# A two-block fp32 model on one core: LRU weights split one product ahead, pairs of second-memory products in one bank, attention tables built in the LRU, priority for the last norm tile, mask products of 64 columns

## The chip, the cores and the metric

The kernel runs as one program on one core of a Trainium2 chip and computes a whole two-block model with a batch of one. The metric is the device time of one execution in microseconds (us), median of three runs. TensorE is called PE in the profile, VectorE DVE, ScalarE ACT, GpSimd POOL, and the queue that issues most loads SP.

## What is computed

The input has 1024 tokens of 1024 values. The first block is a mixer (spatial gating, a state-space branch, attention to a memory), a residual and a layer norm. The second block is the part that matters here:

```python
h = rms_norm(x, norm_mix)
lru_in, lru_gate, q, k, v, g_lru, g_attn = split(h @ w_in)
xc = causal_depthwise_conv(lru_in, conv_w, conv_b)
hr = rg_lru(xc, lru_wa, lru_ba, lru_wx, lru_bx, lru_lambda)   # a scan over the tokens
y_lru = (gelu(lru_gate) * hr) @ w_lru_o
o_attn = diff_attention(q, k, v, cos, sin, ...)               # 8 heads, 2 maps each
x = x + (sigmoid(g_lru) * y_lru + sigmoid(g_attn) * (o_attn @ w_attn_o)) @ w_out
x = x + memory_cross_attention_2(x, mem, ...)                 # kv = rms_norm(mem) @ w_ckv
x = x + hierarchical_moe(rms_norm(x, norm_ffn), ...)
```

In `diff_attention` queries and keys are normed per head and partly rotated by tables `cos` and `sin`, and a query sees the keys of its own chunk of 64 tokens and of all chunks before it. Query tiles have 128 tokens, so in the last key tile the first 64 queries must not see the last 64 keys.

## The kernel before, in words

Every product is kept near fp32 by a split: an operand is rounded into a high part on ACT (`Copy` to fp32r) and the rest is taken on DVE (`x - hi`), and `mm3` (L172 to L176) makes three matmuls of it: high by high, and the two mixed ones. `stream` and `load_split` load a weight by SP into a raw buffer (a ring of two in the LRU), and `split` (L168) makes `wh` on ACT and `wl` on DVE; `wh` and `wl` have four buffers each.

The program is written stage by stage, and the tile framework's scheduler orders the instructions of each engine by priority and by when it expects their inputs. The order in the code is the priority, unless `high_priority` raises it or `behind` lowers it; `issue_after` adds an order against a named instruction. Each engine then runs its list strictly in that order, and waits at an instruction whose inputs are late.

Three stages are touched.

- `ln1` (L957). Eight token tiles: product, residual, layer norm, the second block's first norm (`xnt`), then `finish()` transposes the tile on PE (L949) and splits it into `xnh` and `xnl`. The last two tiles are finished after the loop. All later products read `xnh` and `xnl`.
- `lru` (L1037). Eight channel blocks c. For each, `proj` makes two products of 48 matmuls of 512 columns: `w_li` of the next block, and `w_lgate` of this one. Then come the gate products (`pg`, with `w_lg2`), tanh, exp and sqrt on ACT, and the scan on DVE. In `proj` the weight is loaded and split when its product is written, so just ahead of it. Between the blocks the generator `mem2` (L1671) advances by one step: it makes keys and values of the second memory by eight products of 24 matmuls with 256 columns (`w_ckv`, four column blocks n, two token tiles t), each in a PSUM tile `pj` of the pool `pm2`, which has one buffer. ACT evicts each to `kn` (keys, n below 2) or `kv` (values). Keys are normed and transposed back on PE into a tile `pt` that shares that one buffer (L1697). The memory itself is split into `mh` and `ml` by eight ACT and eight DVE instructions, which are ordered behind `ln_end`, the last square and the last scaling of `ln1`.
- `attention` (L1166). At its start POOL builds the two rotation tables `rot` (L1174 to L1184, five instructions each), POOL and DVE fill the mask operands `ma` and `mb` (L1190 to L1193), and PE makes the first key and value products. `norm_rope` norms on DVE (`nr`), takes two products with `rot` (`rp`), and `transposed` puts the result through PE (L1249). `unit_qk` makes the scores of one query tile, head and map: matmuls L1487 and L1488, then a mask matmul L1490 that adds a large negative number. It writes 256 columns, of which 64 are not zero; there are 4 x 8 x 2 x 2 = 128 of them.

```python
            def proj(src, w=None):
                w = w or self.stream(W, src, [128, 8, 128])
                ps = PJ.tile([128, 2, 512], F32, name="pj", tag="pj")
...
        for n in range(4):
            w = [self.stream(W, A["w_ckv"][n, j], [128, 4, 256]) for j in range(2)]
            for t in range(2):
                ps = PS.tile([128, 2, 128], F32, name="pj", tag="pj")
```

Of the kernel before, what the change touches and what calls it, by code (L numbers as in the profile page):

```python
# [11 lines left out]
F32 = mybir.dt.float32  # L12
F32R = mybir.dt.float32r
BF = mybir.dt.bfloat16
# [9 lines left out]
LN_EPS = 1e-5  # L24
# [105 lines left out]
class Model:  # L130
# [813 lines left out]
    def transpose_split(self, src, PT, hi, lo):  # L944

        for q in range(2):
# [3 lines left out]
            self.split(hi[:, 4 * q:4 * q + 4], lo[:, 4 * q:4 * q + 4], pt)  # L950
# [6 lines left out]
    def ln1(self):  # L957
# [4 lines left out]
        with self.pool("lnw1") as LW, self.pool("lny", side="right") as NW, self.pool("ln", side="right") as N, self.pool("lnps", bufs=2, space=PSUM) as PO, \  # L962
# [3 lines left out]
            def finish():  # L966
                i, xn = last.pop(0)
                self.transpose_split(xn, PT, self.xnh[:, :, i * 128:(i + 1) * 128],
                                     self.xnl[:, :, i * 128:(i + 1) * 128])
# [18 lines left out]
            for i in range(8):  # L988
# [17 lines left out]
                r = N.tile([128, 2, 512], F32, name="r", tag="r")  # L1006
                st = N.tile([128, 2, 6], F32, name="st", tag="st", bufs=2)
                for n in range(2):
                    self.stt(r[:, n], xr[:, n * 512:(n + 1) * 512], ALPHA, ps[:, n], OP.mult, OP.add)
                    nc.vector.bn_stats(out=st[:, n], in_=r[:, n])  # L1010
                if i < 6:
                    nxx.append(load_x(i + 2))
                mv = N.tile([128, 8], F32, name="mv", tag="mv", bufs=2)
                nc.vector.bn_aggr(out=mv[:, 0:2], in_=st)
                self.ts(mv[:, 2:3], mv[:, 1:2], LN_EPS, OP.add)
                self.rsqrt(mv[:, 3:4], mv[:, 2:3], 1)
                r1 = r.rearrange("p a b -> p (a b)")
                self.ts(r1, r1, mv[:, 0:1], OP.subtract, mv[:, 3:4], OP.mult)
                x1 = N.tile([128, 1024], F32, name="x1t", tag="x1t")
                self.tt(x1, r1, lg, OP.mult)  # L1020
                self.tt(x1, x1, lb, OP.add, nc.vector if i == 7 else nc.gpsimd)
                nc.gpsimd.dma_start(out=self.x1[i], in_=x1)
                xn = N.tile([128, 1024], F32, name="xnt", tag="xnt", bufs=2)
                sq = self.act(xn, x1, AF.Square, accum=mv[:, 4:5])
                self.ts(mv[:, 5:6], mv[:, 4:5], 1.0 / 1024, OP.mult, EPS, OP.add)
# [1459 lines left out]
```

## Time and profile before

| what | value |
|---|---|
| time, median of 3 runs | 2520.61 us (2520.1 to 2521.86) |
| time of the profiled execution | 2518.23 us |
| its span in the profile | 2516.5 us |
| PE busy | 2364.3 us, 94% of the span |
| DVE, ACT, POOL busy | 1772.8, 1246.2, 504.8 us |
| `ln1`, its product to the last transposes | about 300 to 466 us |
| LRU | about 446 to 712 us |
| attention | about 712 to 1455 us |

The profiled execution has 1.7 us around its span and lies 2.4 us under the median. Matmuls are pipelined: a matmul of 512 columns is shown with 0.39 us and one of 256 columns with 0.28, but they start every 0.23 and 0.12 us, so the starts are to be read, and the idle time in brackets, not the durations. In a row of a timeline the bracket tells how long the engine had been idle and what released it. PEclk is the granted clock of TensorE in the stretch as a share of full speed; a record can stand at full or at half.

### The profile page before, as it was taken

The page shows a single profiled execution, that of the slowest core. Times are in us where ns is not written, and L with a number is a line of the kernel's source. Part 1 is how long each engine was busy: PE and PEld are TensorE (multiplying, and loading weights), DVE is VectorE, ACT ScalarE, POOL GpSimd, SP SyncE. Part 2 cuts the span into 40 slices and gives each one's busy share as a digit, 9 for nine tenths or more (in the row PEclk, how much of TensorE's full clock was granted, in tenths as well). Part 3 has the DMA queues.
Part 4 walks back from the last instruction along what each step waited for, and adds up shares of the span by engine and source line. Part 5 has one row for each costly group of instructions (what it writes and reads, how often), then busy time and mean ns, then how long its engine had stood idle before and what let it go on. Part 6 is the DMA issues. An engine that isn't in the chain of part 4 may idle for free. (4 is left out here: it accounts for less than half of the span.)

```text
span 2516.5 us, 34506 instructions
## 1 busy us (share of the span) xinstructions
PE 2364.3 (94%) x13016; PEld 1951.4 (78%) x13016; DVE 1772.8 (70%) x3221; ACT 1246.2 (50%) x1850; POOL 504.8 (20%) x362
## 2 busy tenths in 40 slices
PE   8999989989999999999899899999988999988887
PEld 6888868777889898898798778888876777666665
DVE  9667767676775666666666744236658999988887
ACT  5344532453645545455455522124435777766664
POOL 1011114100021021021121100000002333355542
PEclk9999999999999999999999999999988999999999
DMA  6322353312111111110111466532158998999995
GB/s 222 95 70 63 116 187 115 122 69 91 63 68 55 64 35 40 62 51 34 53 49 40 141 204 220 173 138 80 72 217 308 376 373 306 366 338 336 334 338 183
DMA packets 103834, 394.29 MB, mean 157 GB/s; under 512 B 14129, under 2 KB 33073, under 8 KB 79089
## 3 DMA queue, kind: packets, MB, share of 16 engines
q1 hardware_dynamic: 85008, 335.18, 37.8%
q0 software_dynamic: 18656, 56.88, 7.1%
q8 instruction: 104, 1.70, 0.3%
q14 instruction: 66, 0.53, 0.1%
HBM read 339.07 MB, written 61.31 MB: 159 GB/s over the span
## 5 line engine op out<-in xcount | busy, mean ns | idle before, releaser
L166 DVE TENSOR_TENSOR wl<-raw,wh 128x2048 fp32r<-128x2048 f32 (+2 forms) x310 | 566.0, 1839 | 120.0 <-ACT wh L154 119.6
L154 ACT ACTIVATE wh<-raw 128x2048 fp32r<-128x2048 f32 (+2 forms) x310 | 479.6, 1556 | 290.4 <-PE pj L175 87.3
L2248 POOL DMA_INDIRECT out<-y,lsti x32 | 175.2, 5475 | 331.4 <-DVE y L162 281.3
L175 PE MATMUL pg<-wl,xh 128*96 128x512 f32 x512 | 205.6, 402 | 30.1 <-DVE wl L166 29.9
L174 PE MATMUL pj<-wh,xnh 128*128 128x256 f32 x768 | 221.5, 289 | 3.2 <-ACT pc L154 2.7
L176 PE MATMUL pj<-wh,xnl 128*128 128x256 f32 x768 | 217.7, 284 | 0.0
L175 PE MATMUL pj<-wl,xnh 128*128 128x256 f32 x768 | 217.4, 283 | 0.0
L176 PE MATMUL pg<-wh,xl 128*96 128x512 f32 x512 | 201.7, 394 | 0.0
L174 PE MATMUL pg<-wh,xh 128*96 128x512 f32 x512 | 198.3, 396 | 1.0 <-ACT wh L154 1.0
L174 PEld LDWEIGHTS pj<-wh,xnh 128*128 128x128 f32 x768 | 145.4, 189 | 6.2 <-ACT pc L154 4.8
L175 PEld LDWEIGHTS pj<-wl,xnh 128*128 128x128 f32 x768 | 145.5, 189 | 0.0
L176 PEld LDWEIGHTS pj<-wh,xnl 128*128 128x128 f32 x768 | 145.3, 189 | 0.0
L179 POOL TENSOR_TENSOR ss<-ss,mhalf 128x4 f32<-128x4 f32 (+1 forms) x68 | 74.2, 1092 | 343.6 <-DVE ss L163 254.0
L175 PEld LDWEIGHTS pg<-wl,xh 128*96 128x96 f32 x512 | 82.8, 162 | 76.4 <-DVE wl L166 44.5
L154 ACT ACTIVATE e<-sc,st,ss 128x1024 f32<-128x1024 f32 (+7 forms) x128 | 105.6, 829 | 64.5 <-DVE st L158 47.6
L174 PEld LDWEIGHTS pg<-wh,xh 128*96 128x96 f32 x512 | 82.9, 162 | 37.3 <-ACT wh L154 1.4
L174 PE MATMUL pj<-xnh,wh 128*128 128x512 f32 x256 | 103.4, 405 | 7.3 <-ACT wh L154 7.0
L176 PEld LDWEIGHTS pg<-wh,xl 128*96 128x96 f32 x512 | 83.1, 162 | 32.7
L175 PE MATMUL pj<-xnl,wh 128*128 128x512 f32 x256 | 102.4, 401 | 1.3 <-DVE xnl L166 1.3
L174 PE MATMUL pg<-xnh,wh 128*128 128x512 f32 x256 | 103.1, 403 | 0.4 <-ACT kv L154 0.3
L176 PE MATMUL pj<-xnh,wl 128*128 128x512 f32 x256 | 101.9, 400 | 0.3 <-DVE wl L166 0.3
L176 PE MATMUL pg<-xnh,wl 128*128 128x512 f32 x256 | 102.1, 399 | 0.0
(997 smaller groups left out, 6429.5 us busy)
## 6 DMA issues: line engine op xcount, KB each, us to landing
raw<-in_w_gu SPq DMA_DIRECT2D x128, 1024.0 KB, 7.7
raw<-in_w_dn SPq DMA_DIRECT2D x64, 1024.0 KB, 9.6
raw<-in_w_out SPq DMA_DIRECT2D x16, 512.0 KB, 4.5
ta<-tg POOLq DMA_DIRECT2D x32, 256.0 KB, 2.4
t<-ta SPq DMA_DIRECT2D x14, 512.0 KB, 4.3
raw<-in_w_ga SPq DMA_DIRECT2D x12, 512.0 KB, 3.5
raw<-in_w_v SPq DMA_DIRECT2D x12, 512.0 KB, 3.4
xraw<-in_xT SPq DMA_DIRECT2D x8, 512.0 KB, 8.9
```

Source lines behind the costliest of these rows:

```text
L154: return self.nc.scalar.activation(out=out, in_=in_, func=func, **kw)
L166: return (eng or self.nc.vector).tensor_tensor(out=out, in0=a, in1=b, op=op)
L174: mm(ps, l[0], r[0], start=start, stop=False)
L175: mm(ps, l[0], r[1], start=False, stop=False)
L176: mm(ps, l[1], r[0], start=False, stop=stop)
L179: self.nc.gpsimd.tensor_tensor(out=out, in0=in_, in1=self.mhalf[:, :w], op=OP.pow)
L2248: return nc.gpsimd.indirect_dma_start(out=self.out, out_offset=bass.IndirectOffsetOnAxis(ap=u["row"], axis=0), in_=u["y"], in_offset=None, ...
```

## The change

1. LRU: `proj` takes its weight from a list and first starts the load and split of the next one, so each weight is split a whole product ahead.
2. `mem2`: the two token tiles of a block n share one PSUM tile (`pair`) of 2 x 256 columns in the one buffer; the transposes `pt` move to the pool of the gate products, which has three buffers.
3. `attn_const` is called in block c = 1 of the LRU and not after it, and now builds the first table (`rot[1]`, for keys) and the mask operands too; the table for queries is still built at the attention's start. `ma` and `mb` are bf16, `mb` has 64 columns, and all four memsets are on DVE.
4. `ln1`: the norm chain of tile 7 is written under high priority, and `ln_end` is now the last split of the last `finish()`, so what is ordered behind it (the split of the memory, `attn_const`) comes later.
5. The mask product writes 64 columns instead of 256, with bf16 operands.

```diff
     def split(self, hi, lo, src, eng=None):
-        self.act(hi, src, AF.Copy)
-        self.tt(lo, src, hi.bitcast(F32), OP.subtract, eng)
+        return self.act(hi, src, AF.Copy), self.tt(lo, src, hi.bitcast(F32), OP.subtract, eng)
...
-                r = N.tile([128, 2, 512], F32, name="r", tag="r")
...
-                sq = self.act(xn, x1, AF.Square, accum=mv[:, 4:5])
...
-                xs = self.stt(xn, x1, mv[:, 6:7], nm, OP.mult, OP.mult)
+                with self.tc.high_priority(URGENT) if i == 7 else nullcontext():
+                    r = N.tile([128, 2, 512], F32, name="r", tag="r")
...
+                    self.stt(xn, x1, mv[:, 6:7], nm, OP.mult, OP.mult)
                 last.append((i, xn))
-            self.ln_end = sq, xs
             finish()
-            finish()
+            self.ln_end = finish()
...
-            beside = self.mem2(W, M, PM)
+            beside = self.mem2(W, M, PM, PG)
...
-            def proj(src, w=None):
-
-                w = w or self.stream(W, src, [128, 8, 128])
+            srcs = [A["w_li"][1], A["w_lgate"][0]]
+            for c in range(1, 8):
+                srcs += [A["w_li"][c + 1], A["w_lgate"][c]] if c < 7 else [A["w_lgate"][7]]
+            ws = []
+
+            def ahead():
+                if srcs:
+                    ws.append(self.stream(W, srcs.pop(0), [128, 8, 128]))
+
+            def proj(w=None):
+
+                w = w or ws.pop(0)
+                ahead()
...
+                if c == 1:
+                    with self.tc.issue_after(self.ln_end[1].ins):
+                        self.attn_const(self.at0)
                 next(beside, None)
...
-            with self.tc.issue_after(self.ln_end[1].ins):
-                self.attn_const(self.at0)
...
+        self.rotation(T, 1)
+
+        self.ma = ma = T.tile([128, 128], BF, name="ma")
+        self.mb = mb = T.tile([128, 64], BF, name="mb")
+        nc.vector.memset(ma, 0.0)
+        nc.vector.memset(mb, 0.0)
+        nc.vector.memset(ma[0:1, 0:64], 1.0)
+        nc.vector.memset(mb[0:1], -(2.0 ** 100))
+
+    def rotation(self, T, j):
...
-            ma = T.tile([128, 128], F32R, name="ma")
-            mb = T.tile([128, 384], F32R, name="mb")
-            nc.gpsimd.memset(ma.bitcast(F32), 0.0)
-            nc.gpsimd.memset(mb.bitcast(F32), 0.0)
...
+            self.rotation(T1, 0)
...
                 if last:
-                    nc.tensor.matmul(base[:, o + n - 256:o + n], ma, mb[:, 128:384] if i == 0 else mb[:, 0:256],
-                                     start=False, stop=True)
+
+                    end = 128 if i == 0 else o + n
+                    nc.tensor.matmul(base[:, end - 64:end], ma, mb, start=False, stop=True)
...
-            pt = PS.tile([128, 2, 128], F32, name="pt", tag="pj")
+            pt = PG.tile([128, 2, 128], F32, name="pt", tag="pg")
...
+            pair = PS.tile([128, 2, 2, 128], F32, name="pj", tag="pj")
             for t in range(2):
-                ps = PS.tile([128, 2, 128], F32, name="pj", tag="pj")
+                ps = pair[:, t]
```

What this does to the order of instructions shows at three places. The new file is longer at the top of what changed, so its line numbers differ by one to 19.

**DVE at the end of `ln1`.** `xnt` is the scaled last tile, `xnl` the low parts of its transposes, for which PE waits; `ml` belongs to the second memory. Before:

```order
L163 TENSOR_SCALAR st<-st 128x2
L163 TENSOR_SCALAR mv<-mv 128x1
L158 SCALAR_TENSOR_TENSOR xnt<-x1t,mv,row_norm_mix 128x1024
L158 SCALAR_TENSOR_TENSOR ml<-raw,cols,mh 128x256 x3
L162 TENSOR_SCALAR sub<-cols 128x1
L162 TENSOR_SCALAR lamn<-lamc 128x1
L1158 COPY gcol<-cols 128x2
L158 SCALAR_TENSOR_TENSOR ml<-raw,cols,mh 128x256 x5
L166 TENSOR_TENSOR xnl<-ptr,xnh 128x4x128
L1159 MEMSET gcol 16x2
L1160 MEMSET gcol 16x2
L166 TENSOR_TENSOR xnl<-ptr,xnh 128x4x128
```

With the change:

```order
L163 TENSOR_SCALAR st<-st 128x2
L166 TENSOR_TENSOR wl<-raw,wh 128x1024
L163 TENSOR_SCALAR mv<-mv 128x1
L158 SCALAR_TENSOR_TENSOR xnt<-x1t,mv,row_norm_mix 128x1024
L166 TENSOR_TENSOR xnl<-ptr,xnh 128x4x128 x2
L162 TENSOR_SCALAR sub<-cols 128x1
L162 TENSOR_SCALAR lamn<-lamc 128x1
L1170 COPY gcol<-cols 128x2
L1182 MEMSET ma 128x64
L1183 MEMSET mb 128x32
L158 SCALAR_TENSOR_TENSOR ml<-raw,cols,mh 128x256 x2
```

The two `xnl` stand directly behind `xnt`, the eight `ml` behind them, and a weight split `wl` (for the LRU's third product of `w_li`) stands ahead of the last square's result `mv`.

**ACT in the LRU.** `wh` of 1024 columns is a weight's high part, `xi` the eviction of a `w_li` product, `kn` and `kv` the evictions of the second memory's products, `tr`, `ti`, `tau` and `ex` the gates of a channel block. Around the first pair of second-memory products, before:

```order
L154 ACTIVATE tr<-pg,hb 128x512
L154 ACTIVATE kn<-pj,st 128x256
L154 ACTIVATE sq<-kn 128x256
L154 ACTIVATE tr<-pg,hb 128x512
L154 ACTIVATE xch<-xc 128x1024
L154 ACTIVATE q<-q 128x1024
L154 ACTIVATE tau<-tr,lpar 128x1024
L154 ACTIVATE ex<-tr,lpar 128x1024
L154 ACTIVATE wh<-raw 128x1024
L154 ACTIVATE kn<-pj,st 128x256
L154 ACTIVATE wh<-raw 128x1024
```

The same with the change:

```order
L154 ACTIVATE wh<-raw 128x1024
L154 ACTIVATE xi<-pj 128x1024
L154 ACTIVATE kn<-pj,st 128x256
L154 ACTIVATE sq<-kn 128x256
L154 ACTIVATE wh<-raw 128x1024
L154 ACTIVATE kn<-pj,st 128x256
L154 ACTIVATE wh<-raw 128x1024
L154 ACTIVATE sq<-kn 128x256
L154 ACTIVATE ti<-pg,hb 128x512 x2
L154 ACTIVATE kv<-pt,cols 128x2x128
L154 ACTIVATE wh<-raw 128x256
```

The weights' splits now stand ahead of the gates and of `tau` and `ex`, and the first eviction `kn` stands behind a weight's split and `xi`. Around the third pair, with the change:

```order
L154 ACTIVATE tr<-pg,hb 128x512
L154 ACTIVATE xch<-xc 128x1024
L154 ACTIVATE ti<-pg,hb 128x512 x2
L154 ACTIVATE tau<-tr,lpar 128x1024
L154 ACTIVATE ex<-tr,lpar 128x1024
L154 ACT_TABLE_LOAD
L154 ACTIVATE sq<-tau,lpar 128x1024
L154 ACTIVATE wh<-raw 128x1024
L154 ACTIVATE xi<-pj 128x1024
L154 ACTIVATE kv<-pj,st 128x256
L154 ACTIVATE wh<-raw 128x1024
L154 ACTIVATE kv<-pj,st 128x256
```

The first eviction `kv` of that pair stands behind the whole gate work of a block, a weight's split and `xi`.

**POOL at the attention's start.** `rot_6608` is the table for keys, `rot_6614` the one for queries; `ta` is a store of a gate. Before:

```order
L166 TENSOR_TENSOR rot_6608<-ropec,grow 128x8x8
L166 TENSOR_TENSOR rot_6608<-ropes,grow 128x8x8 x2
L166 TENSOR_TENSOR rot_6608<-ropec,grow 128x8x8
L166 TENSOR_TENSOR rot_6614<-ropec,grow 128x8x8
L166 TENSOR_TENSOR rot_6614<-ropes,grow 128x8x8 x2
L166 TENSOR_TENSOR rot_6614<-ropec,grow 128x8x8
L1190 MEMSET ma 128x128
L1191 MEMSET mb 128x384
L1275 DMA ta_4786<-tg 128x512
L1184 TENSOR_SCALAR rot_6608<-rot_6608 128x8x8
L1184 TENSOR_SCALAR rot_6614<-rot_6614 128x8x8
L1275 DMA ta_4786<-tg 128x512
```

With the change, where `rot_6616` is the table for queries:

```order
L166 TENSOR_TENSOR rot_6616<-ropec,grow 128x8x8
L166 TENSOR_TENSOR rot_6616<-ropes,grow 128x8x8 x2
L166 TENSOR_TENSOR rot_6616<-ropec,grow 128x8x8
L1292 DMA ta_4786<-tg 128x512
L1196 TENSOR_SCALAR rot_6616<-rot_6616 128x8x8
L1292 DMA ta_4786<-tg 128x512
```

The table for keys and the two memsets are gone from here; its five instructions now stand at the end of `ln1`, behind the reciprocal root `mv` of tile 7 and ahead of the store of that tile.

## Rows read from the trace of the kernel before

**Rows 1.** The page's busy time of each engine

```profile
PE 2364.3 (94%) x13016; PEld 1951.4 (78%) x13016; DVE 1772.8 (70%) x3221; ACT 1246.2 (50%) x1850; POOL 504.8 (20%) x362
```

**Rows 2.** Busy time by stretch: us, PE, PEld, DVE, ACT, POOL, PEclk, DMA share, GB/s

```profile
455.00:470.00 15.00, 10.28 (x38) 7.40 (x37) 10.19 (x25) 7.36 (x16) 1.90 (x5) 0.77 0.44 146
...
515.00:535.00 20.00, 16.27 (x82) 13.08 (x81) 18.40 (x23) 16.29 (x21) 1.59 (x4) 0.91 0.25 86
...
723.00:735.00 12.00, 8.21 (x57) 8.00 (x56) 7.18 (x17) 2.55 (x6) 6.58 (x16) 0.86 0.22 85
```

**Rows 3.** PE in order of time, last norm tile: start, us, instruction, [idle before <-releaser]

```profile
462.13 1.06 PE L949 MATMUL ptr<-ident,xnt 128*128 128x128 f32 x8 [3.14 <-DVE xnt L158]
463.50 1.22 PE L174 MATMUL pj<-xnh,wh 128*128 128x512 f32 x2 [0.30 <-ACT xnh L154]
466.00 0.80 PE L175 MATMUL pj<-xnl,wh 128*128 128x512 f32 x1 [1.28 <-DVE xnl L166]
```

**Rows 4.** VectorE in order of time, the same stretch

```profile
454.97 1.23 DVE L166 TENSOR_TENSOR x1t<-r,row_ln_g 128x1024 f32<-128x1024 f32 x1
...
463.28 2.06 DVE L158 SCALAR_TENSOR_TENSOR ml<-raw,cols,mh 128x256 fp32r<-128x256 f32 x5
465.26 0.69 DVE L166 TENSOR_TENSOR xnl<-ptr,xnh 128x512 fp32r<-128x512 f32 x1
```

**Rows 5.** Who PE waited for, 470 to 712: us in total, times, longest

```profile
PE pj L174 <- ACT wh L154: 7.0, 4, 3.0
PE pj L174 <- ACT kv L154: 3.3, 2, 1.9
PE pt L1699 <- ACT kv L154: 0.7, 1, 0.7
```

**Rows 6.** ScalarE in order of time, the middle of the LRU

```profile
555.06 1.27 ACT L154 ACTIVATE ti<-pg,hb 128x512 f32<-128x512 f32 x2
...
559.14 1.04 ACT L154 ACTIVATE xch<-xc 128x1024 fp32r<-128x1024 f32 x1
...
560.44 1.24 ACT L154 ACTIVATE tau<-tr,lpar 128x1024 f32<-128x1024 f32 x1
...
562.82 1.28 ACT L154 ACT_TABLE_LOAD   x1
564.12 1.15 ACT L154 ACTIVATE sq<-tau,lpar 128x1024 f32<-128x1024 f32 x1
565.17 1.04 ACT L154 ACTIVATE wh<-raw 128x1024 fp32r<-128x1024 f32 x1
```

**Rows 7.** VectorE in order of time, the attention's start

```profile
721.40 0.68 DVE L166 TENSOR_TENSOR nr<-pc,ss 128x512 f32<-128x512 f32 x1
723.41 2.48 DVE L166 TENSOR_TENSOR nr<-pc,ss 128x512 f32<-128x512 f32 x1 [1.32 <-POOL ss L179]
725.81 0.33 DVE L166 TENSOR_TENSOR rp<-nr,rot 128x64 f32<-128x64 f32 x1
...
727.65 0.26 DVE L166 TENSOR_TENSOR rp<-nr,rot 128x64 f32<-128x64 f32 x1 [0.91 <-POOL rot L1184]
```

**Rows 8.** PE in order of time, the attention's start

```profile
728.29 0.66 PE L1249 MATMUL pt<-ident,nr 128*128 128x128 f32 x4 [3.79 <-DVE nr L166]
```

**Rows 9.** ScalarE in order of time, the attention's start

```profile
728.90 0.60 ACT L154 ACTIVATE tg<-pg 128x512 f32<-128x512 f32 x1 [2.23 <-DMA ta<-tg]
```

**Rows 10.** PE in order of time, a mask product (L1490)

```profile
777.01 0.28 PE L1490 MATMUL sc<-mb,ma 128*128 128x256 f32 x1
777.13 0.28 PE L1487 MATMUL sc<-kh,qs 128*128 128x256 f32 x1
```

**Rows 11.** PE in order of time, a bf16 product among f32 ones

```profile
1813.99 0.18 PE L2098 MATMUL prk<-cacc,one 128*128 128x32 bf16 x1
...
1814.33 0.39 PE L176 MATMUL pq<-wcq1h,xl 128*128 128x512 f32 x1
1814.56 0.39 PE L174 MATMUL pq<-wcq2h,xh 128*128 128x512 f32 x1
```

More of the change, by code (lines that the diff above doesn't have):

```diff
@@ L949, in transpose_split @@
                 self.nc.tensor.transpose(pt[:, i], src[:, (4 * q + i) * 128:(4 * q + i + 1) * 128], self.ident)
-            self.split(hi[:, 4 * q:4 * q + 4], lo[:, 4 * q:4 * q + 4], pt)
+            last = self.split(hi[:, 4 * q:4 * q + 4], lo[:, 4 * q:4 * q + 4], pt)
+        return last
     def row(self, pool, name, width):
@@ L967, in finish @@
                 i, xn = last.pop(0)
-                self.transpose_split(xn, PT, self.xnh[:, :, i * 128:(i + 1) * 128],
-                                     self.xnl[:, :, i * 128:(i + 1) * 128])
+                return self.transpose_split(xn, PT, self.xnh[:, :, i * 128:(i + 1) * 128],
+                                            self.xnl[:, :, i * 128:(i + 1) * 128])
             ring = (NW, "raw", 4)
@@ L1005, in ln1 @@
                     finish()
-                r = N.tile([128, 2, 512], F32, name="r", tag="r")
[L1007 to L1021, printed above, removed]
@@ L1022, in ln1 @@
-                nc.gpsimd.dma_start(out=self.x1[i], in_=x1)
-                xn = N.tile([128, 1024], F32, name="xnt", tag="xnt", bufs=2)
-                sq = self.act(xn, x1, AF.Square, accum=mv[:, 4:5])
-                self.ts(mv[:, 5:6], mv[:, 4:5], 1.0 / 1024, OP.mult, EPS, OP.add)
-                self.rsqrt(mv[:, 6:7], mv[:, 5:6], 1)
-                xs = self.stt(xn, x1, mv[:, 6:7], nm, OP.mult, OP.mult)
+                with self.tc.high_priority(URGENT) if i == 7 else nullcontext():
+                    r = N.tile([128, 2, 512], F32, name="r", tag="r")
+                    st = N.tile([128, 2, 6], F32, name="st", tag="st", bufs=2)
+                    for n in range(2):
+                        self.stt(r[:, n], xr[:, n * 512:(n + 1) * 512], ALPHA, ps[:, n], OP.mult, OP.add)
+                        nc.vector.bn_stats(out=st[:, n], in_=r[:, n])
+                    if i < 6:
+                        nxx.append(load_x(i + 2))
+                    mv = N.tile([128, 8], F32, name="mv", tag="mv", bufs=2)
+                    nc.vector.bn_aggr(out=mv[:, 0:2], in_=st)
+                    self.ts(mv[:, 2:3], mv[:, 1:2], LN_EPS, OP.add)
+                    self.rsqrt(mv[:, 3:4], mv[:, 2:3], 1)
+                    r1 = r.rearrange("p a b -> p (a b)")
+                    self.ts(r1, r1, mv[:, 0:1], OP.subtract, mv[:, 3:4], OP.mult)
+                    x1 = N.tile([128, 1024], F32, name="x1t", tag="x1t")
+                    self.tt(x1, r1, lg, OP.mult)
+                    self.tt(x1, x1, lb, OP.add, nc.vector if i == 7 else nc.gpsimd)
+                    nc.gpsimd.dma_start(out=self.x1[i], in_=x1)
+                    xn = N.tile([128, 1024], F32, name="xnt", tag="xnt", bufs=2)
+                    self.act(xn, x1, AF.Square, accum=mv[:, 4:5])
+                    self.ts(mv[:, 5:6], mv[:, 4:5], 1.0 / 1024, OP.mult, EPS, OP.add)
+                    self.rsqrt(mv[:, 6:7], mv[:, 5:6], 1)
+                    self.stt(xn, x1, mv[:, 6:7], nm, OP.mult, OP.mult)
@@ L1075, in conv @@
                 return xc
-            first = [proj(A["w_li"][c], None if c else self.w0) for c in range(2)]
+            first = [proj(None if c else self.w0) for c in range(2)]
             for g in first:
@@ L1082, in lru @@
             self.w0p.__exit__(None, None, None)
-            ahead = next(first[1])
+            second = next(first[1])
             for c in range(8):
@@ L1086, in lru @@
                 if c < 7:
-                    nxt = conv(c + 1, ahead if c == 0 else [*proj(A["w_li"][c + 1])][1])
-                ps = [*proj(A["w_lgate"][c])][1]
+                    nxt = conv(c + 1, second if c == 0 else [*proj()][1])
+                ps = [*proj()][1]
                 xch = T.tile([128, 1024], F32R, name="xch", tag="xch")
```

32 lines of the change are left out of this document (15 added, 17 removed).

## The prediction

> **What bounds the kernel now.** I read the page first: PE is busy for 2364.3 of the span's 2516.5 us [rows 1]. The work is one chain of PE products, so an edit off PE is worth only the PE idle time that it ends, and an edit on PE the distance between starts that it saves. Next I read PE's idle time in order of time, and PE's waits summed by releaser, in the stages that the change touches. At the end of `ln1` PE waits 3.14 us for `xnt`, then 0.30 for `xnh` and 1.28 for `xnl` [rows 3]. In the LRU it waits 7.0 us for weights' `wh`, 3.3 for `kv`, and twice 0.7 before the transposes `pt` [rows 5]. At the attention's start it waits 3.79 us for `nr` [rows 8].
>
> Third, the granted clock by stretch. It falls behind such waits: 0.91 over 20 us at 515 to 535, 0.77 over 15 us at 455 to 470, 0.86 over 12 us at 723 to 735 [rows 2], where the full clock (2.4 GHz) gives 1.00 and the other level (1.2 GHz) half of that. The share that is missing is the time lost: 0.09 x 20 = 1.8 us, 0.23 x 15 = 3.4 us, 0.14 x 12 = 1.7 us. The LRU has three such stretches like the one shown, each behind a wait for `wh`.
>
> The sum is made against the profiled execution, 2518.2 us (a span of 2516.5 and 1.7 around it). It lies 2.4 us under the median of 2520.6, so that much is added at the end. About 0.2%, 5.0 us, is what a measurement of this kernel can tell from no change.
>
> **End of `ln1`.** Five `ml` (2.06 us) run just ahead of the first `xnl` [rows 4], while the transposes are long there. The change puts both `xnl` ahead of all `ml`, and the same holds for `mh` and `xnh` on ACT. The waits of 0.30 and 1.28 us go [rows 3]: -1.6 us. The 3.14 us stay: in the order, high priority moves no instruction of the chain against another. What comes into the chain is the weight split `wl` between `st` and `mv`, where DVE has nothing to do until ACT's square is ready; I cost it at nothing, and if ACT made its `wh` late, `wl` (as long as `x1t`, 1.23 us [rows 4]) would push the chain by up to that. `ml` and `mh` are now later, but the second memory's products stand behind 123 matmuls of 0.23 us, over 25 us of cover. The half clock stays, as its wait stays. Bounds: 0 (the split costs as much as the waits give) and -1.6 - 3.4 = -5.0; I take -1.6, the rows' own number.
>
> **LRU, what goes.** `wh` is late because ACT, in order, first runs `tau` (1.24), `ex`, a table load (1.28) and `sq` (1.15) [rows 6]. A weight that is split one product ahead has a product of 48 x 0.23 = 11 us as cover. So the 7.0 us go. The waits for `kv` and before `pt` come from the one buffer that `pt` shares with the products; with `pt` in the other pool the 3.3 and 1.4 us go too. That is 11.7 us, and the three half-clock stretches behind them, 5.4 us: 17.1 in all.
>
> **LRU, what comes.** The two products of a pair share a bank, so the second waits until ACT has read the first. Ahead of that read stand, in the new order, a weight's `wh` and `xi`; PE meanwhile has the rest of the pair's first product. In the third pair (n = 2) more stands ahead. Its `tr` is released 25 matmuls (25 x 0.23 = 5.8 us) before PE ends the `w_li` product. ACT then needs `tr` (half of the `ti` pair, 0.6), `xch` 1.04, `ti` 1.27, and `tau` to `sq` 564.12 + 1.15 - 560.44 = 4.8 [rows 6], 7.7 us, and is 1.9 late. Then follow `wh` 1.04 [rows 6], `xi` of the same size, and `kv` at some 0.5, 2.6 us, of which PE covers nine matmuls at 0.12, 1.1. PE waits 1.9 + 2.6 - 1.1 = 3.4 us. In the second pair the queue ahead is only `wh`, `xi` and `kn`: 2.6 - 1.1 = 1.5 us. In the first, PE has nearly a whole product left, and only the read itself is bare, 0.6. In the fourth the evictions stand alone: 0. Together 5.5 us, and one stretch at half clock behind the longest, 1.8: 7.3. **LRU: -17.1 + 7.3 = -9.8 us.** Bounds: all three pairs as short as the first, 1.8 and no half clock, gives -15; two more pairs like the third (5.2 each) give about 0.
>
> **Attention's start.** PE waits for `nr`. DVE's `nr` took 2.48 us beside POOL's `rot` instructions, against 0.68 for the same instruction just before; then `rp` ran at 725.81, and the next `rp` only at 727.65, behind two memsets and the wait for POOL's last scaling of the table [rows 7]. Without these the second `rp` follows at 725.81 + 0.33 = 726.14, 1.5 us sooner; with four `rot` instructions beside `nr` in place of eight, it may be more. A new wait takes part of this back: `tg` waits for the DMA of the tile before it (2.23 us [rows 9]), and in the new order the products behind the first eight transposes need `tg`; its DMA is issued behind the four `rot`. I take -1.6 with the half clock staying. Bounds: 0, and -1.6 - 1.7 = -3.3.
>
> **The mask.** There are 128 such products. Each starts 0.12 us before the next matmul [rows 10]. The trace has a short bf16 product between f32 ones: from its start at 1813.99 to the second f32 matmul at 1814.33 there are 0.34 us, and a full f32 distance is 1814.56 - 1814.33 = 0.23 [rows 11]. So the short product still costs 0.11 us; the weights of the matmul behind it must come in. The saving is 128 x (0.12 - 0.11) = 1.3 us; I take -1.0. Bounds: 0, and in proportion to the columns 128 x 0.12 x 3/4 = -11.5.
>
> The Trainium skill ("TensorE: Matmul & The Clock Gate", Back-to-back issue gap) gives an isolated product of up to 64 columns a gap of about 25 ns and one of 256 columns 262 cycles. By that rule the mask term would be an estimated -11; [rows 11] speaks against it in a stream with weight loads, and the same section says that the formula under-counts at few columns.
>
> **Sum:** -1.6 - 9.8 - 1.6 - 1.0 = -14.0; 2518.2 - 14.0 = 2504.2, and with the 2.4 us of the median **2506.6**. The three stages left (out projection, second memory, experts) have the same instructions; the attention's are permuted a little, which I cost at 0 with 3 us either way.
>
> **Rivals.**
>
> (A) *The shared bank gives back what the split ahead gains.* If the second and the fourth pair wait like the third, 5.2 us with the half clock, the new waits are 3 x 5.2 + 0.6 = 16.2 and the LRU gains 0.9. With -4.2 from the rest that is -5.1: 2515.5. For it: the eviction stands behind `wh` and `xi` in all of the first three pairs. Against: only the third has `tau` to `sq` ahead as well.
>
> (B) *The shared bank costs more, and the kernel is slower.* ACT and PE run through the LRU together, and if every one of the four pairs met ACT with the whole queue from `tau` to `wh` ahead (565.17 + 1.04 - 560.44 = 5.8 us [rows 6]) and then half clock, a pair would cost 7.6, four 30.4. Less 17.1, that is +13.3, and with -4.2 elsewhere +9.1: 2529.7. It is slower from (17.1 + 4.2) / 4 = 5.3 us a pair on, and by over 5 us from 6.6. Against it: the order shows the queue in that form once.
>
> (C) *The mask goes with its columns*: 10.5 us more, 2496. Against it [rows 11].
>
> (D) *POOL slows the last norm chain.* The five instructions of the first table now stand right behind tile 7's reciprocal root, and DVE's scaling and `x1t` run then. In the one place where such instructions ran beside DVE's `nr`, it took 2.48 in place of 0.68 us [rows 7], 3.6 times. The two on the chain, 1.23 for `x1t` [rows 4] and some 0.8 for the scaling, would gain 2.0 x 2.6 = 5.2 us at most, all of it in PE's wait: 2511.8. POOL needs only about 2 us for the five, so a part of that is likelier. The Trainium skill ("GPSIMD Engine Reference", 1. Specifications) says that POOL's SBUF interface is shared with VectorE and contended by instructions with two SBUF inputs. [...]
>
> (E) The change might not do what it says: for `high_priority` that is so, as the chain's order is the same before and after. The other parts show in the order.
>
> **How the numbers follow.** The forecast has 0.64, (A) 0.14, (B) 0.07, (C) 0.06, (D) 0.09. (A) lies on the edge of 0.2%, at 5.1 us, so I count it as no change; the forecast, (C) and (D) are faster, 0.79, and (B) slower. The range runs from (C)'s edge, 2496, past (D) and (A) to 2516.5, the LRU's upper bound of 0 with the other terms as taken; (B) and the tails stay out.
>
> **What would show it.** In the changed profile: the waits for `xnh` and `xnl` gone at 463 to 466 and the 3.14 kept; no PE wait for `wh` in the LRU; waits for `kn` and `kv` in the middle of the pairs, the longest some 3.4 us, in the third; one LRU stretch at half clock and not three; the wait before the first transposes of the attention near 2 us; the mask's distance 0.11. I am wrong if the waits for `kn` and `kv` sum to over 10 us, if the mask's distance falls to 0.03, or if `x1t` of tile 7 takes over 2 us.

## The result, and the profile after

The change takes 2502.28 us (median of 4 runs, 2500.42 to 2504.78), against 2521.24 us of the kernel before in the same session. The ratio is 0.993, with a 95% interval of 0.9916 to 0.9943: 14 to 21 us faster, about 18. Forecast were 2506.6 us, 14.0 less than before, in a range of 2496 to 2516.5.

The profiled execution of the change took 2504.78 us, the slowest of its four, while that of before was under its median. So the two traces differ by only 13.5 us of span. First the page of the change, part 1 (busy us, share of the span, instructions):

```profile
span 2503.0 us, 34498 instructions
...
PE 2361.7 (94%) x13016; PEld 1934.8 (77%) x13016; DVE 1770.6 (71%) x3223; ACT 1246.3 (50%) x1850; POOL 503.7 (20%) x360
```

PE is as busy as in [rows 1] (2361.7 against 2364.3 us), and the span is 13.5 us shorter: what went is idle time and half clock. Where it went is read from the starts of the same instructions in both traces, PE in order of time, before:

```profile
711.43 0.28 PE L174 MATMUL pj<-wh,xnh 128*128 128x256 f32 x1
...
776.77 0.28 PE L1487 MATMUL sc<-kh,qs 128*128 128x256 f32 x1
...
1437.15 0.31 PE L1487 MATMUL sc<-kh,qs 128*128 128x320 f32 x1
...
2502.74 0.39 PE L176 MATMUL pd<-wh,ahl 128*96 128x512 f32 x1
```

and with the change, together with the last transposes of `ln1` and the next matmuls:

```profile
460.55 1.56 PE L948 MATMUL ptr<-ident,xnt 128*128 128x128 f32 x8 [3.32 <-DVE xnt L158]
461.94 1.22 PE L173 MATMUL pj<-xnh,wh 128*128 128x512 f32 x2
462.96 0.63 PE L174 MATMUL pj<-xnl,wh 128*128 128x512 f32 x1
...
694.00 0.28 PE L173 MATMUL pj<-wh,xnh 128*128 128x256 f32 x1
...
758.07 0.28 PE L1504 MATMUL sc<-kh,qs 128*128 128x256 f32 x1
...
1420.31 0.31 PE L1504 MATMUL sc<-kh,qs 128*128 128x320 f32 x1
...
2489.70 0.39 PE L175 MATMUL pd<-wh,ahl 128*96 128x512 f32 x1
```

| stretch | before | after | difference |
|---|---|---|---|
| start of the program to the last tile's transposes | 462.13 | 460.55 | -1.6 |
| from there to the attention's first product (LRU) | 249.3 | 233.45 | -15.85 |
| attention's first product to its first scores | 65.3 | 64.1 | -1.3 |
| first scores to last scores | 660.4 | 662.2 | +1.9 |
| last scores to the last expert product | 1065.6 | 1069.4 | +3.8 |

The first line is not the change's doing, which touches nothing there before tile 7: between 215 and 225 us the clock is 0.83 in the trace of before and 1.00 in this one, 1.7 us. Of the last line a net 1.7 us are the clock as well: 3.4 us were lost in the router's stretch (below), and 1.7 won right behind the attention, where the clock was 0.82 (1437 to 1465 us) and is 0.88 (1420 to 1448). Its other 2 us stay open. The line above it goes with 0.99 and 0.98 over 660 us, a digit that stands for up to 6.6 us. The stretches by time show it for the change (us, PE, PEld, DVE, ACT, POOL, PEclk, DMA share, GB/s):

```profile
215.00:225.00 10.00, 9.10 (x47) 7.35 (x48) 9.48 (x23) 6.60 (x13) 3.01 (x1) 1.00 0.16 63
...
453.00:468.00 15.00, 11.68 (x49) 9.12 (x48) 11.48 (x29) 7.72 (x16) 4.36 (x9) 0.89 0.40 125
468.00:694.00 226.00, 221.01 (x1045) 182.31 (x1044) 179.44 (x171) 130.23 (x151) 9.14 (x19) 1.00 0.26 86
...
758.00:1420.00 662.00, 634.10 (x4254) 564.23 (x4254) 429.78 (x1093) 330.24 (x685) 97.74 (x112) 0.98 0.16 53
...
1833.00:1910.00 77.00, 58.39 (x288) 45.38 (x287) 50.34 (x128) 29.92 (x38) 12.70 (x10) 0.78 0.69 255
```

and for before, where the last two answer to the last two there:

```profile
215.00:225.00 10.00, 9.06 (x37) 7.26 (x38) 8.35 (x21) 5.74 (x13) 2.99 (x1) 0.83 0.17 64
...
470.00:711.00 241.00, 228.24 (x1053) 186.93 (x1052) 180.47 (x171) 128.41 (x150) 10.61 (x19) 0.98 0.23 79
...
776.00:1437.00 661.00, 633.39 (x4261) 579.06 (x4261) 430.23 (x1096) 331.77 (x685) 99.42 (x112) 0.99 0.16 53
...
1850.00:1925.00 75.00, 56.48 (x294) 43.33 (x293) 52.07 (x128) 31.09 (x37) 12.48 (x10) 0.82 0.73 265
```

In the LRU the clock went from 0.98 to 1.00 and PE's busy share from 228 of 241 to 221 of 226 us. In the router's stretch it was 0.82 and is 0.78, which is 77 x 0.22 - 75 x 0.18 = 3.4 us lost in a stage that the change does not touch. PE's waits in the LRU by releaser (us in total, times, longest):

```profile
PE pj L173 <- ACT kv L154: 3.0, 1, 3.0
PE pj L173 <- ACT kn L154: 1.7, 2, 1.1
...
PE pg L173 <- ACT kv L154: 0.2, 1, 0.2
```

The 7.0 us for `wh` and the waits before `pt` of [rows 5] are gone. What came are the waits in the middle of the pairs, 1.7 us for `kn` (0.6 and 1.1) and 3.0 for `kv`, against 0.6, 1.5 and 3.4 that were worked out. At the end of `ln1` the waits for `xnh` and `xnl` of [rows 3] have no bracket any more, and 3.3 us stay.

The attention's start, PE in order of time, against [rows 8]:

```profile
708.10 1.42 PE L1266 MATMUL pt<-ident,nr 128*128 128x128 f32 x8 [1.04 <-DVE nr L166]
710.55 0.58 PE L173 MATMUL pj<-wh,xnh 128*128 128x256 f32 x1 [1.04 <-ACT tg L154]
```

The wait for `nr` fell from 3.79 to 1.04 us, and the wait for `tg` that was expected behind the transposes is there, 1.04.

### The profile page after: what moved, and what is told of

Read it like the earlier page. It is cut to its first block, busy times and chain, and to the rows that moved or that the text cites. A ratio compares the mean times of both kernels' runs of the same rounds, so it can differ in the third digit from the quotient of the medians.

```text
span 2503.0 us, 34498 instructions
## 1 busy us (share of the span) xinstructions
PE 2361.7 (94%) x13016; PEld 1934.8 (77%) x13016; DVE 1770.6 (71%) x3223; ACT 1246.3 (50%) x1850; POOL 503.7 (20%) x360
## 5 line engine op out<-in xcount | busy, mean ns | idle before, releaser
L166 DVE TENSOR_TENSOR wl<-raw,wh 128x2048 fp32r<-128x2048 f32 (+3 forms) x310 | 566.3, 1840 | 109.7 <-ACT wh L154 108.4
L154 ACT ACTIVATE wh<-raw 128x2048 fp32r<-128x2048 f32 (+3 forms) x310 | 480.0, 1558 | 240.6 <-PE pj L174 65.8
L174 PE MATMUL pg<-xnl,wh 128*128 128x512 f32 x256 | 101.5, 397 | 0.0
```

What stands on the lines that cost most here:

```text
L154: return self.nc.scalar.activation(out=out, in_=in_, func=func, **kw)
L166: return (eng or self.nc.vector).tensor_tensor(out=out, in0=a, in1=b, op=op)
L174: mm(ps, l[0], r[1], start=False, stop=False)
```

## The experiments

In the tables, LRU waits are the sum of PE's waits between 465 and 705 us, without those for `pc` and `xnl`, which lie outside the LRU. In the row of e6_two_banks, 2.4 of the 2.7 us are a wait of the attention's first gate product. A run is compared with the kernel before on its own chip.

| run | what it is | ratio to before | 95% interval | LRU waits, us |
|---|---|---|---|---|
| (before) | | 1 | | 12.9 |
| r0_change | the change again | 0.9931 | 0.9916 to 0.9947 | 4.9 |
| e1_split_late | change without the split ahead | 0.9932 | 0.9918 to 0.9945 | 3.8 |
| e2_no_pair | change without the pair, `pt` in the products' buffer | 0.9938 | 0.9925 to 0.9952 | 5.7 |
| e8_neither | both undone | 0.9977 | 0.9967 to 0.9987 | 11.5 |
| e9_pt_moved | both undone, `pt` in the gates' pool | 0.9925 | 0.9912 to 0.9938 | 3.8 |
| e10_pt_only | before, `pt` in the gates' pool | 0.9940 | 0.9928 to 0.9953 | 3.9 |
| e6_two_banks | change, two banks for the products | 0.9954 | 0.9939 to 0.9969 | 2.7 |
| e4_tables_late | change, tables as before | 0.9946 | 0.9926 to 0.9966 | 4.9 |
| e5_ln_before | change, `ln1` as before | 0.9939 | 0.9926 to 0.9952 | 4.9 |
| e3_mask_only | before, mask of 64 columns | 0.9987 | 0.9978 to 0.9995 | 14.1 |
| e12_mask_256 | change, mask of 256 columns | 0.9939 | 0.9923 to 0.9954 | 4.9 |
| e11_pt_tg2 | e9_pt_moved with two `tg` | 0.9932 | 0.9916 to 0.9948 | 3.8 |

### The change again (r0_change)

No edit.

> The change as it is, beside the kernel before on the same chip, as the measure for the runs that undo one part of it. Expected is a ratio of 0.993 with 0.001 either way (about -17 us). If a part of the gain came only from where the half-clock stretches of the first profile happened to fall, the ratio is nearer to 0.9945 (-14 us, the sum of the parts).

Measured: 0.9931 (0.9916 to 0.9947), 2504.12 us against 2522.19. The first result holds, at 17 us. Six executions of this one kernel lie between 2500.05 and 2509.48, so two single executions say little about 3 us.

### The split ahead undone (e1_split_late)

```diff
             def proj(w=None):
 
-                w = w or ws.pop(0)
-                ahead()
+                w = w or self.stream(W, srcs.pop(0), [128, 8, 128])
```

> The change with one part undone: each LRU weight is loaded and split when its own product is written, as before. My theory (the split ahead is the largest part): PE's waits for wh in the LRU come back with about 7 us and one to three half-clock stretches of 1.8 us, so it is 8 to 12 us slower than the change: ratio to the kernel before 0.9965 to 0.998. Rival (the waits for kv and pt in the one bank were the cause and wh only came next in the queue): the waits for wh stay under 2 us and the ratio is that of the change, 0.993.

Measured: 0.9932, the change's own ratio. My theory falls. PE's waits in the LRU (us, times, longest):

```profile
PE pj L173 <- ACT kn L154: 3.1, 3, 2.0
...
PE pj L175 <- DVE wl L166: 0.5, 1, 0.5
PE pg L173 <- ACT kv L154: 0.2, 1, 0.2
```

There is no wait for `wh` at all, and the waits in the middle of the pairs are 3.1 us and not 4.7. The split ahead is not what ended the waits for weights, as long as the other LRU part is there.

### The pair undone (e2_no_pair)

```diff
-            pt = PG.tile([128, 2, 128], F32, name="pt", tag="pg")
+            pt = PS.tile([128, 2, 128], F32, name="pt", tag="pj")
...
-            pair = PS.tile([128, 2, 2, 128], F32, name="pj", tag="pj")
...
-                ps = pair[:, t]
+                ps = PS.tile([128, 2, 128], F32, name="pj", tag="pj")
```

> The change with one part undone: each second-memory product has its own tile in the one buffer, and the transposes pt share that buffer, as before. My theory (the pair removes 4.7 us of waits and brings 4.7): the waits for kn (0.6 and 1.1) and kv (3.0) in the middle of the pairs are replaced by waits of the same kind at every product and before pt, 4 to 7 us in all; ratio within 0.001 of the change, 0.993 to 0.994. Rival (sharing a bank is a net cost): the LRU's waits fall under 2 us and it is 3 us faster than the change, 0.992.

Measured: 0.9938, within 0.001 of the change. The waits, 5.7 us in all, are of the forecast kind:

```profile
PE pj L173 <- ACT wh L154: 2.1, 2, 1.1
PE pj L173 <- ACT kv L154: 1.1, 2, 0.6
...
PE pt L1717 <- ACT kn L154: 0.6, 1, 0.6
...
PE pj L175 <- DVE wl L166: 0.5, 1, 0.5
```

The split ahead alone takes the 7.0 us for `wh` of [rows 5] to 2.1. So each part alone does nearly the whole of it, and undoing one of them tells nothing about the other. That asked for the next two runs.

### Both undone (e8_neither), and the move of pt by itself (e9_pt_moved)

e8_neither is both edits above. e9_pt_moved leaves `pt` in the gates' pool:

```diff
-                w = w or ws.pop(0)
-                ahead()
+                w = w or self.stream(W, srcs.pop(0), [128, 8, 128])
...
-            pair = PS.tile([128, 2, 2, 128], F32, name="pj", tag="pj")
...
-                ps = pair[:, t]
+                ps = PS.tile([128, 2, 128], F32, name="pj", tag="pj")
```

> The change with both LRU parts undone: weights split when their product is written, each second-memory product with its own tile in the one buffer, and pt in that buffer. Either part alone undone left the ratio at 0.993 to 0.994. Theory 1 (the two parts stand in for each other): with both undone the LRU's waits come back to about 12 us with three half-clock stretches, and the ratio is 0.998 (13 to 17 us slower than the change). Theory 2 (neither matters, the gain comes from the order that the tables in block 1 or the end of ln1 give): the LRU's waits stay near 5 us and the ratio stays at 0.993.

> Of the LRU parts only one is left: the transposes pt are in the gate products' pool. Weights are split when their product is written and each second-memory product has its own tile in the one buffer. Theory 1 (it is the pair that lets the second-memory products run early and free the four wh buffers): LRU waits 7 us or more, ratio 0.995 to 0.998. Theory 2 (it is the move of pt that frees the buffer): LRU waits under 6 us, ratio 0.993 to 0.994.

Measured: e8_neither 0.9977 (0.9967 to 0.9987), with the waits back at 11.5 us and a mean clock between 470 and 700 us of 0.98 as before, where the change has 1.00:

```profile
PE pj L173 <- ACT wh L154: 4.5, 3, 2.5
PE pj L173 <- ACT kv L154: 3.3, 2, 1.9
PE pj L175 <- DVE wl L166: 2.1, 2, 1.8
```

Theory 1 of that run holds: the two parts stand in for each other, and together they are worth 0.9977 - 0.9931, some 12 us. What is left in e8_neither, the end of `ln1`, the tables and the mask, is worth some 6 us by its ratio. e9_pt_moved gives 0.9925 (0.9912 to 0.9938) with the same waits as e1_split_late, 3.1 us for `kn` and 0.5 for `wl`. So of the pair and the move of `pt`, which came in one part of the diff, it is the move that counts. The pair adds nothing that these runs can tell.

### The move of pt on the kernel before (e10_pt_only)

```diff
-    def mem2(self, W, T, PS):
+    def mem2(self, W, T, PS, PG):
...
-            pt = PS.tile([128, 2, 128], F32, name="pt", tag="pj")
+            pt = PG.tile([128, 2, 128], F32, name="pt", tag="pg")
```

> The kernel before with one line changed in effect: the second memory's transposes pt are in the gate products' pool. Nothing else of the change. Theory (the move of pt is what ends the LRU's waits): LRU waits fall from 12.9 to 4 to 6 us and one or no half-clock stretch is left in the LRU: 10 to 13 us faster than before, ratio 0.995 to 0.996. Rival (it needs the later end of ln1 or the tables in block 1 as well): LRU waits stay over 9 us, ratio 0.998 or more.

Measured: 0.9940 (0.9928 to 0.9953), 15 us of the change's 17 from one tile in another pool. The LRU waits are 3.9 us, and the mean clock between 470 and 700 us is 1.00. How it comes is seen on ACT in order of time, at the first block of second-memory products:

```profile
516.97 0.47 ACT L154 ACTIVATE kn<-pj,st 128x256 f32<-128x256 f32 x1 [0.16 <-PE pj L176]
...
519.24 1.06 ACT L154 ACTIVATE wh<-raw 128x1024 fp32r<-128x1024 f32 x1 [1.34 <-PE pj L176]
...
522.57 0.45 ACT L154 ACTIVATE kn<-pj,st 128x256 f32<-128x256 f32 x1
...
535.18 1.24 ACT L154 ACTIVATE tau<-tr,lpar 128x1024 f32<-128x1024 f32 x1
```

`wh` at 519.24 is released by PE's product on second-memory weights, the last reader of the buffer that it reuses. It now runs between the two evictions `kn`, and `tau` comes 16 us behind it. In [rows 6] `wh` stands behind `tau`, the table load and `sq`. There, with `pt` in the products' own buffer, PE runs the second product of a block behind the gate products and waits for the bank first. Before, PE in order of time:

```profile
560.60 0.39 PE L174 MATMUL pj<-wh,mh 128*128 128x256 f32 x1 [1.89 <-ACT kv L154]
```

This product is the last reader of its block's weights, and on ACT the split of the next weight stands behind the gates. With `pt` elsewhere the two products follow each other, and the buffer is free in time, without a split a product ahead. That the scheduler places the split late because it expects the buffer late is inferred from the two orders; no run shows its reckoning.

### Two banks for the products (e6_two_banks)

```diff
-                self.pool("pj2", bufs=2, space=PSUM) as PJ, self.pool("pg2", bufs=3, space=PSUM) as PG, \
-                self.pool("pm2", bufs=1, space=PSUM) as PM:
+                self.pool("pj2", bufs=2, space=PSUM) as PJ, self.pool("pg2", bufs=2, space=PSUM) as PG, \
+                self.pool("pm2", bufs=2, space=PSUM) as PM:
...
-            pair = PS.tile([128, 2, 2, 128], F32, name="pj", tag="pj")
...
-                ps = pair[:, t]
+                ps = PS.tile([128, 2, 128], F32, name="pj", tag="pj")
```

> The change with the second memory's products in two banks, one each, and the gate products and pt in two banks in place of three. Theory (the waits in the middle of the pairs are for the read of the shared bank): the waits for kn and kv of 4.7 us go; if two banks are enough for the gates, it is 3 to 5 us faster than the change, ratio 0.991 to 0.992. Rival (the gates need the third bank): new waits of pg for ti and tr of 3 us or more, ratio 0.993 or higher.

Measured: 0.9954 (0.9939 to 0.9969), some 6 us slower than the change, though the two intervals touch. The waits in the middle of the pairs went, as expected, and none for `ti` or `tr` came. The loss is at the LRU's end:

```profile
PE pj L173 <- ACT pc L154: 3.7, 2, 3.2
PE pg L173 <- ACT kv L154: 2.4, 1, 2.4
```

The last eviction `kv` holds the bank for the attention's first gate product (2.4 us). `pc` comes 3.2 us late: on ACT the gates of the last channel block, from `ti` at 689.73 to the end of `sq` at 698.56 us, run ahead of it almost without a pause. At the attention's start the waits for `nr` and `tg` are 1.9 and 1.8 us as well, against 1.04 each. Neither theory had this: by these rows PE, which waits less in the LRU, is through with it sooner than ACT, and meets ACT's queue at the stage's end.

### The tables late (e4_tables_late)

```diff
-                if c == 1:
-                    with self.tc.issue_after(self.ln_end[1].ins):
-                        self.attn_const(self.at0)
...
+            with self.tc.issue_after(self.ln_end[1].ins):
+                self.attn_const(self.at0)
...
-        self.rotation(T, 1)
...
-            self.rotation(T1, 0)
+            self.rotation(T1, 1)
+            self.rotation(T1, 0)
```

> The change with one part undone: attn_const behind the LRU, both rotation tables and the mask operands of 64 columns at the attention's start. Expected: the wait of 3.8 us before the first transposes comes back in place of 1.0 and 1.0, one half-clock stretch stays, 1 to 3 us slower than the change, ratio 0.9935 to 0.9945. Rival (the tables' place also sets the LRU's order): the LRU's waits change by more than 2 us.

Measured: 0.9946, with an interval (0.9926 to 0.9966) that takes in the change. The waits at the attention's start, though, are plain, PE in order of time and DVE's `nr` beside the eight `rot` instructions:

```profile
708.42 1.97 PE L1265 MATMUL pt<-ident,nr 128*128 128x128 f32 x8 [2.85 <-DVE nr L166]
```

```profile
704.48 2.76 DVE L166 TENSOR_TENSOR nr<-pc,ss 128x512 f32<-128x512 f32 x1 [1.32 <-POOL ss L178]
...
707.77 0.26 DVE L166 TENSOR_TENSOR rp<-nr,rot 128x64 f32<-128x64 f32 x1 [0.36 <-POOL rot L1194]
```

2.85 us (3.8 were expected) in place of 1.04 and 1.04, 0.8 us of PE time. The LRU's waits are those of the change, so the rival falls.

### The end of ln1 as before (e5_ln_before)

```diff
-                with self.tc.high_priority(URGENT) if i == 7 else nullcontext():
+                with nullcontext():
...
-                    self.act(xn, x1, AF.Square, accum=mv[:, 4:5])
+                    sq = self.act(xn, x1, AF.Square, accum=mv[:, 4:5])
...
-                    self.stt(xn, x1, mv[:, 6:7], nm, OP.mult, OP.mult)
+                    xs = self.stt(xn, x1, mv[:, 6:7], nm, OP.mult, OP.mult)
...
-            finish()
-            self.ln_end = finish()
+            self.ln_end = sq, xs
+            finish()
+            finish()
```

> The change with one part undone: no priority for tile 7's norm chain, and ln_end as before, so the memory's split is ordered only behind the square and the scaling. Expected: the waits of 0.3 and 1.3 us for xnh and xnl come back behind the wait of 3.3, and the half clock behind them lasts 6.8 and not 3.4 us (1.7 more): 1.5 to 3.3 us slower, ratio 0.9935 to 0.9945. Rival (something else moved ml behind xnl): no such wait, and the ratio is 0.993.

Measured: 0.9939 (0.9926 to 0.9952), and the waits for `xnl` do not come back: the rival holds. DVE and SP in order of time show why:

```profile
461.19 1.27 DVE L158 SCALAR_TENSOR_TENSOR ml<-raw,cols,mh 128x256 fp32r<-128x256 f32 x3
...
463.14 0.69 DVE L166 TENSOR_TENSOR xnl<-ptr,xnh 128x512 fp32r<-128x512 f32 x1
...
464.68 0.86 DVE L158 SCALAR_TENSOR_TENSOR ml<-raw,cols,mh 128x256 fp32r<-128x256 f32 x2
```

```profile
452.82 6.38 SPq L1697 DMA_DIRECT2D raw<-in_mem2T  x2
```

Four of the eight `ml` stand ahead of `xnl` again (three of them in the first row), where it was all eight. The load of the memory's second half is issued 6 us behind that of the first, against 1.2 us in the kernel before, since the weight that is split ahead now holds its raw buffer. The other four `ml` have no data yet, and DVE is free when the transposes are done. So this gain also has two causes, each of which is enough: in e1_split_late and e8_neither, which have the new order and no split ahead, PE does not wait for `xnl` either. In e10_pt_only, which has neither, the wait of 1.3 us for `xnl` is there.

### The mask alone (e3_mask_only) and undone (e12_mask_256)

```diff
-            ma = T.tile([128, 128], F32R, name="ma")
-            mb = T.tile([128, 384], F32R, name="mb")
...
+            ma = T.tile([128, 128], BF, name="ma")
+            mb = T.tile([128, 64], BF, name="mb")
...
-                    nc.tensor.matmul(base[:, o + n - 256:o + n], ma, mb[:, 128:384] if i == 0 else mb[:, 0:256],
-                                     start=False, stop=True)
+                    end = 128 if i == 0 else o + n
+                    nc.tensor.matmul(base[:, end - 64:end], ma, mb, start=False, stop=True)
```

The second run is this edit backwards, on the change, and it also puts the filling of the operands back to the attention's start, two of the four fills on POOL.

> The kernel before with only the mask changed: 64 columns and bf16 operands, built where they were. My theory (the weights of the next matmul bind): the distance from the mask product to the next matmul falls from 0.12 to 0.04 us, but that matmul's own distance to the one behind it grows by nearly as much, and the time falls by 0 to 1.5 us: ratio 0.9995, no change that can be told. Rival (the mask goes with its columns): -8 to -11 us, ratio 0.996 to 0.997.

> The change with the mask undone: 256 columns in fp32r, the operands filled at the attention's start as before. The mask alone on the kernel before gave 0.9987 (0.9978 to 0.9995), while the distances of its matmuls sum to no gain. Theory (the mask's columns are free, as the next weights bind; the 0.9987 came from elsewhere in the run): distances mask to next 0.12 and next to its follower back to 0.23 for 512 columns, the same sum, and the ratio is that of the change, 0.9925 to 0.9935. Rival (the mask is worth the 3.3 us of that run): ratio 0.9943 or higher.

PE in order of time with the change, at the same place as [rows 10]:

```profile
758.30 0.20 PE L1509 MATMUL sc<-mb,ma 128*128 128x64 bf16 x1
758.35 0.36 PE L1504 MATMUL sc<-kh,qs 128*128 128x256 f32 x1
758.55 0.28 PE L1505 MATMUL sc<-kl,qs 128*128 128x256 f32 x1
```

The mask product starts 0.05 us before the next matmul, in place of 0.12, and that matmul 0.20 before its own follower, in place of 0.12. Over the 95 mask products of e3_mask_only and before that have no idle time around them and the same neighbours, the distance from the first score matmul to the second one behind the mask is 0.015 us longer on average: in these places nothing was saved. The times do not settle it: 0.9987 (0.9978 to 0.9995) for the mask alone is a larger gain than the 0.9995 expected, and 0.9939 (0.9923 to 0.9954) with it undone lies between the two expectations. In e12_mask_256 the wait for `tg` is also 1.57 us and not 1.04, which the place of the fills can bring without the columns. Nor do the traces settle it. From the first to the last scores e3_mask_only takes 661.1 us and the kernel before 660.4, so the 3.3 us by which its span is shorter lie ahead of the attention; but the clock over these scores is 0.98 against 0.99, a digit that can hide a few us. Whether a part of the 3 us is the mask's stays open.

### Two tg (e11_pt_tg2)

```diff
-                t = T.tile([128, 512], F32, name="tg", tag="tg", bufs=1)
+                t = T.tile([128, 512], F32, name="tg", tag="tg", bufs=2)
```

on e9_pt_moved.

> A version meant to be the best: the change without the split ahead and without the pair, with pt in the gate products' pool (as in e9_pt_moved) and two buffers for tg. Theory: the wait of 1.0 us for tg at the attention's start goes, and with it perhaps the half-clock stretch behind it (1.7): 1 to 3 us faster than e9_pt_moved, ratio 0.9915 to 0.992. Rival (the wait for tg hides another): a wait for pc or nr takes its place and the ratio stays at 0.9925.

Measured: 0.9932 (0.9916 to 0.9948). At the attention's start the waits for `nr` and `tg` fell from 1.1 and 1.0 us in e9_pt_moved to 0.36 and none, so the cause of the 1.0 us was the right one:

```profile
707.25 0.66 PE L1265 MATMUL pt<-ident,nr 128*128 128x128 f32 x4 [0.36 <-DVE nr L166]
```

but the time is not below that of e9_pt_moved (0.9925): the 1 to 3 us expected are less than the runs of two kernels can tell apart. No version beats the change by more than that.

## Why the prediction was right, and where not

- **The time and the sign** were right: -14.0 us forecast, -14 to -21 measured. In the two traces, the terms that the change touches sum to -15.85 - 1.3 = -17.1 us, against -1.6 - 9.8 - 1.6 = -13.0 without the mask. That the spans of the two traces differ by 13.5 us, so near the forecast, is luck: 1.6 us more went ahead of the change's stages, and 5.7 came behind them, in part clock.
- **End of `ln1`.** -1.6 came true, and 3.3 us stay, as said. The half clock behind them did not stay whole: it is 0.89 and not 0.77 over 15 us, 1.8 us better. The reason that the prediction gave, `ml` behind `xnl` by the order, was one of two; e5_ln_before shows that the late raw buffer alone does it.
- **LRU, what goes.** The sum was right, the reason given was not the one that counts: "A weight that is split one product ahead has a product of 48 x 0.23 = 11 us as cover. So the 7.0 us go." The split ahead does take them, to 2.1 (e2_no_pair). But without it they go all the same (e1_split_late), wholly, and they go in the kernel before when only `pt` moves (e10_pt_only). So the change holds two causes that each nearly suffice, and that the term came true is no test of the reason given, and in part luck. I read the wait for `wh` as the place of a split in ACT's queue. That place itself hung on the bank that `pt` shared with the products. I had counted this bank only for the waits for `kv` and before `pt`, 4.7 of the 11.7 us. Nor did each of the three half-clock stretches stand behind a wait for `wh`: in the middle one the clock was 0.88 from 559 to 563 us, behind the 1.89 us for `kv`, and 0.69 from 563 to 567, where the wait for `wh` ended only at 566.26.
- **LRU, what comes.** 0.6, 1.5 and 3.4 us were forecast in the pairs, 0.6, 1.1 and 3.0 measured. The one half-clock stretch behind the longest did not come: 1.8 us better. With the 0.8 us less of waits and the 1.8 us of `ln1`, these are the 4.4 us by which the stretch came out above the forecast.
- **Attention's start.** -1.6 forecast, -1.3 measured, with the waits for `nr` and `tg` both there. The permuted order of the attention was costed at 0 with 3 us either way; it came out as +1.9, with the clock at 0.98 against 0.99.
- **The mask.** -1.0 forecast, nothing seen in the distances, and a gain of a few us not excluded by the times. The distance of 0.11 to the next matmul did not come: it is 0.04 to 0.05, and the cost shows one matmul later. Rival (C), -11 us by the columns, falls with e3_mask_only (0.9987). The Trainium skill ("TensorE: Matmul & The Clock Gate", Back-to-back issue gap) gives an isolated product of up to 64 columns about 25 ns; here its start was 0.04 to 0.05 us ahead of the next, and the matmul behind it paid 0.08 more. The measurement decides: at the 95 places compared, going from 256 to 64 columns saved nothing.
- **Rivals (A) and (B)**, new waits in every pair, fall: only the third pair met the gates' queue. **Rival (D)**, POOL on the norm chain, falls too: `x1t` took 1.23 us as in [rows 4], beside POOL's instructions, and POOL waited (below).

## What to carry to other kernels

Where one PSUM buffer holds a product and also the transposes of its result, the wait can show up far away, as here: on weight buffers that the delayed product still holds, and on the splits queued behind. Ask of a wait for a weight which instruction freed the buffer that it is written into, before blaming the queue that it stands in. When several edits go in together, undo each one and also all of them: two edits that each remove the same wait look worthless one by one.

## What the runs showed of the hardware that was not expected

The cost of POOL beside DVE falls on one or on the other. At the attention's start DVE's `nr` took 2.48 us beside eight `rot` instructions [rows 7], 2.76 in e4_tables_late, and 1.38 beside four in the change; alone it takes 0.68. At the end of `ln1` it was the other way round. With the change, POOL in order of time, then DVE:

```profile
452.31 0.32 POOL L166 TENSOR_TENSOR rot<-ropec,grow 128x64 f32<-128x64 f32 x1
452.59 2.03 POOL L166 TENSOR_TENSOR rot<-ropes,grow 128x64 f32<-128x64 f32 x2
454.59 0.32 POOL L166 TENSOR_TENSOR rot<-ropec,grow 128x64 f32<-128x64 f32 x1
```

```profile
452.36 0.81 DVE L163 TENSOR_SCALAR r<-r,mv 128x1024 f32<-128x1024 f32 x1 [0.44 <-POOL mv L178]
453.21 1.23 DVE L166 TENSOR_TENSOR x1t<-r,row_ln_g 128x1024 f32<-128x1024 f32 x1
```

Two `rot` instructions took 2.03 us, where a pair of the same takes 0.59 in e4_tables_late, and DVE's two ran as long as before, 0.81 and 1.23 us. Spans on POOL are rough in the profile, but this pair took over three times the usual. The Trainium skill ("GPSIMD Engine Reference", 1. Specifications) has POOL's SBUF interface shared with VectorE, and contended by DVE instructions with two SBUF inputs or in a 2-port perf mode. `nr` and `x1t` have two SBUF inputs, so the trace agrees at both places; which engine waits is read here from the rows alone.

The half clock is not the same in two executions of a kernel of one core: the mean granted clock of the six of r0_change goes from 0.979 (2509.48 us) to 0.985 (2500.05 us). It also differs between two kernels where they do the same. Between 215 and 225 us the clock stood at 0.83 before and 1.00 with the change, and in the router's stretch at 0.82 and 0.78 (0.78 again in the trace of r0_change). Executions of one kernel differ by 9 us in r0_change and by 16 in e4_tables_late, so effects of 1 to 3 us were read from the waits, and not from the times.
